# Expert stage of a hybrid RWKV-7/GLA/MoE layer: gates and float32r parts in the copies of w2's sums, scatter within the next pair, other terms of y in the tenth pair, branch in the fourteenth

## Chip, cores and metric

The kernel runs on 1 core of one Trainium2 chip. The metric is the device time of one execution in microseconds (us), the median of several runs. Engines are named as in the profile: PE is TensorE's matmul side and PEld its weight loads, DVE is VectorE, ACT is ScalarE, POOL is GpSimd, SP is SyncE, whose queue issues the weight transfers.

## What is computed

One encoder layer for 256 tokens of width 1024: an RWKV-7 and a GLA mixer, then a top-4-of-32 mixture of experts, each followed by a layer norm of alpha times the residual plus the result. The change lies in the mixture of experts:

```
logits = xt @ router_w + router_b
top_val, top_idx = lax.top_k(logits, 4)
gate = softmax(top_val)
for each expert e, for the tokens that chose it:
    h = xt[tok] @ w1[e] + b1[e]                     # 1024 -> 2048
    gt = minimum(h[:, :1024], 7); up = clip(h[:, 1024:], -7, 7)
    act = (up + 1) * gt * sigmoid(1.702 * gt)
    o = act @ w2[e] + b2[e]                         # 1024 -> 1024
    y[tok] += gate * o
x = layer_norm(alpha * x + y)
```

All 32 experts' weights are float32 and are read from memory once: w1 is 8 MB an expert, w2 4 MB.

## The kernel before

The mixing stage (to about 240 us) ends in the router (`out_route`, `choose`). The expert stage is a loop over 16 **pairs** of experts, `e2` 0 to 15. Each expert takes up to 64 of its tokens, so that the two of a pair fill 128 columns.

Weights arrive through a **ring of ten slots** of 2 MB (`fetch`, L284), filled by SP's queue in the order of the stream: for each pair eight slots of w1 and four of w2. SP issues a transfer only when PE has read the last of what stood in its slot.

Within a pair PE does, in the order of the program:

- **Gather** (L1264): `so`, a 0/1 matrix of tokens by places, times the normalised tokens; ACT (L1099) and DVE (L1100) copy the result out of PSUM to `xg` with the norm's gain.
- **Transposes of sg** (L1286): `so` times the gates is `sg` (DVE); its transpose `sgT` is copied by ACT (L1287).
- **w1** (L1310), 16 instructions a slot, with the bias at L1314; `swiglu` (DVE, ACT) and four transposes (L1090) give `aT`.
- **w2** (L1332), 16 instructions a slot. There is one PSUM bank for its sums (`bo`); ACT copies the lower 64 rows to `oc` (L1334), DVE the upper 64 (L1335), and the second expert's w2 waits for the first's copies.
- **Scatter** (L1339): `sgT` times `oc`, float32, four matmuls of 128x512 in eight instructions, each sum added to `y` by DVE (L1340). It waits for the second expert's copies, and the next pair's gather stands behind it.

`init_y` (L1223 to L1234) writes y's other terms, alpha times the residual and the gate times b2, in pair 0 between the two experts of w2. At pair 6 stands `overflow` (L1120 to L1122): a branch with a loop for experts with more than 64 tokens, which all engines pass, SP among them. From pair 2 on a row of parameters for the last norm lies in `oh` (L1212, on SP's queue, behind `init_y`, which reads the same tile).

In the last pair (15) w2 is read in pieces of 256 columns (L1363): even pieces sum into a bank `o`, odd ones into a bank `x`; ACT copies each to `oq` (L1365), and its scatter (L1368) and DVE's addition to `y` follow. Then come the norm and the output.

A scheduler sets the order of instructions on each engine, by its own estimate of times; it also takes w1's matmuls of the two experts in turn where `xg` comes late.

Of the kernel before, what the change touches and what calls it, by code (L numbers as in the profile page):

```python
# [137 lines left out]
def mix_moe(ctx: ExitStack, tc: tile.TileContext, A, out, dbg=None):  # L138
# [1103 lines left out]

    gained = [None, None]
    for e2 in range(NE // 2):
# [32 lines left out]
        sgT = mo.tile([128, 2, T], F32, name="sgT", tag="sgT")  # L1277
        pb = bank("x")
        for v in range(2):
            for t in range(2):  # L1280
                o = pb[:, v * T + t * 128:v * T + (t + 1) * 128]
                if last:
                    for h in range(2):
                        PE.matmul(o[64 * h:64 * h + 64], lhsT=sg[:, t, v], rhs=ident, start=True, stop=True)
                else:
                    PE.transpose(o, sg[:, t, v:v + 2].rearrange("p a b -> p (a b)"), ident)  # L1286
        S.activation(sgT.rearrange("p a b -> p (a b)"), pb, AF.Copy)  # L1287
        if last:

            ln2 = xres  # L1290
            for i in range(4):
                pb = bank("x")
                for h in range(2):
                    row(pb[:, h * 256:(h + 1) * 256], rt, 2 * i + h)
                S.activation(ln2[:, i // 2, i % 2 * 512:i % 2 * 512 + 512], pb, AF.Copy)
# [146 lines left out]
```

## Time and profile before

| | us |
|---|---|
| median of 3 runs (lowest, highest) | 1199.7 (1198.8, 1199.85) |
| the profiled execution's own time | 1194.37 |
| its span, first to last instruction | 1192.5 |
| PE busy (matmuls; their ends are modelled) | 1092.7 |
| DVE busy | 391.3 |
| ACT busy | 200.6 |
| read from memory | 426.67 MB |

The profiled execution is 5.3 us shorter than the median of the runs. Busy time of PE is no measure of need here: an engine that waits for data only at some slots shows as busy in the rest. The DMA line of the profile's second part is the mean busy share of the core's 16 DMA engines in 40 slices of 29.8 us, in tenths (9 is 90% or more), and the GB/s line under it is what they moved.

### The profile page before, as it was taken

The page shows a single profiled execution, that of the slowest core. Times are in us where ns is not written, and L with a number is a line of the kernel's source. Part 1 is how long each engine was busy: PE and PEld are TensorE (multiplying, and loading weights), DVE is VectorE, ACT ScalarE, POOL GpSimd, SP SyncE. Part 2 cuts the span into 40 slices and gives each one's busy share as a digit, 9 for nine tenths or more (in the row PEclk, how much of TensorE's full clock was granted, in tenths as well). Part 3 has the DMA queues.
Part 4 walks back from the last instruction along what each step waited for, and adds up shares of the span by engine and source line. Part 5 has one row for each costly group of instructions (what it writes and reads, how often), then busy time and mean ns, then how long its engine had stood idle before and what let it go on. Part 6 is the DMA issues. An engine that isn't in the chain of part 4 may idle for free.

```text
span 1192.5 us, 14141 instructions
## 1 busy us (share of the span) xinstructions
PE 1092.7 (92%) x5964; PEld 528.8 (44%) x5964; DVE 391.3 (33%) x792; ACT 200.6 (17%) x368; POOL 83.9 (7%) x75
## 2 busy tenths in 40 slices
PE   8889899999999999999899999999899999998995
PEld 5679787643434343433333333333333333333443
DVE  7767976424222221221212222212222222222125
ACT  5544322111011111110101010110101010101111
POOL 4605610010000000000000000000000000000001
PEclk9879999998999999999999999999999999999998
DMA  9211364689799999999989999999999999999991
GB/s 336 115 71 72 142 255 166 249 346 428 285 429 428 428 429 427 427 428 429 425 357 430 425 429 429 427 426 428 429 428 428 427 428 427 428 426 428 426 400 43
DMA packets 36201, 428.68 MB, mean 359 GB/s; under 512 B 3947, under 2 KB 6276, under 8 KB 9382
## 3 DMA queue, kind: packets, MB, share of 16 engines
q1 hardware_dynamic: 35362, 426.41, 85.5%
q10 hardware_dynamic: 772, 1.32, 0.3%
q8 instruction: 48, 0.79, 0.3%
q14 instruction: 19, 0.16, 0.0%
HBM read 426.67 MB, written 1.05 MB: 359 GB/s over the span
## 4 chain that ended last, share of the span: by engine, by line
PE 28%; DMA 19%; DVE 2%; ACT 1%; issue 0%; DVEq 0%; ACTq 0%
DMA slot<-w 19%; PE bg L1310 13%; PE bo L1332 5%; PE bx L1264 4%; PE bx L1339 3%; DVE oc L1335 1%; PE bx L1368 1%; ACT oc L1334 1%; PE bx L1363 1%; PE bo L1363 1%; PE bx L1090 0%; PE bx L1286 0%; PE bx L1217 0%; DVE y L1391 0%; PE bg L1314 0%
## 5 line engine op out<-in xcount | busy, mean ns | idle before, releaser
L1310 PE MATMUL bg<-slot,xg 128*64 128x512 f32 x2048 | 462.0, 596 | 0.0
L1310 PEld LDWEIGHTS bg<-slot,xg 128*64 128x64 f32 x2048 | 140.7, 137 | 250.8 <-issue 236.2
L1332 PE MATMUL bo<-slot,aT 128*64 128x512 f32 x960 | 218.4, 601 | 35.0 <-DVE oc L1335 16.3
L1332 PEld LDWEIGHTS bo<-slot,aT 128*64 128x64 f32 x960 | 68.1, 138 | 168.4 <-issue 114.8
L1082 DVE TENSOR_SCALAR gt<-bg 128x512 f32<-128x512 f32 x32 | 22.1, 691 | 284.7 <-PE bg L1314 284.7
L1264 PEld LDWEIGHTS bx<-so,xres 128*128 128x128 f32 x512 | 67.8, 196 | 49.4 <-issue 46.4
L1335 DVE COPY oc<-bo 64x512 f32<-64x512 f32 x30 | 20.8, 694 | 205.2 <-ACT oc L1334 205.1
L1264 PE MATMUL bx<-so,xres 128*128 128x128 f32 x512 | 79.4, 292 | 1.1 <-DVEq L1121 1.1
L1100 DVE TENSOR_SCALAR xg<-bx,cst 128x128 f32<-128x128 f32 x64 | 26.2, 410 | 162.0 <-PE bx L1264 111.6
L1339 PE MATMUL bx<-oc,sgT 128*128 128x512 f32 x120 | 55.5, 605 | 21.3 <-DVE oc L1335 21.3
L1083 ACT ACTIVATE up<-gt 128x512 f32<-128x512 f32 x32 | 20.1, 629 | 312.1 <-DVE gt L1082 312.1
L1410 POOL TENSOR_TENSOR y<-y,xres 128x512 f32<-128x512 f32 x1 | 1.4, 1442 | 917.9 <-ACT y L1409 917.9
L1099 ACT ACTIVATE xg<-bx,cst 128x128 f32<-128x128 f32 x64 | 28.6, 457 | 173.8 <-PE bx L1264 170.8
L401 PE MATMUL bp<-xth,whi 128*128 128x256 f32 x144 | 45.0, 313 | 6.9 <-DVE slot L430 6.9
L1340 DVE TENSOR_TENSOR y<-bx,y 128x512 f32<-128x512 f32 x60 | 41.5, 692 | 25.8 <-PE bx L1339 25.8
L1334 ACT ACTIVATE oc<-bo 64x512 f32<-64x512 f32 x30 | 17.7, 591 | 186.9 <-PE bo L1332 179.5
L403 PE MATMUL bp<-xth,wlo 128*128 128x256 f32 x144 | 43.7, 305 | 3.6 <-DVE wlo L391 3.6
L1339 PEld LDWEIGHTS bx<-oc,sgT 128*128 128x128 f32 x120 | 21.6, 189 | 56.0 <-DVE oc L1335 34.5
L402 PE MATMUL bp<-xtl,whi 128*128 128x256 f32 x144 | 43.5, 303 | 0.0
L391 DVE TENSOR_TENSOR wlo<-slot,whi 128x512 fp32r<-128x512 f32 x37 | 35.7, 974 | 19.0 <-ACT whi L388 18.9
L388 ACT ACTIVATE whi<-slot 128x512 fp32r<-128x512 f32 x50 | 31.2, 629 | 49.6 <-PE bp L402 27.2
L1092 ACT ACTIVATE aT<-bx 128x512 f32<-128x512 f32 x32 | 19.1, 597 | 121.5 <-PE bx L1090 121.4
(419 smaller groups left out, 1020.6 us busy)
## 6 DMA issues: line engine op xcount, KB each, us to landing
slot<-w SPq DMA_DIRECT2D x188, 2048.0 KB, 34.1
slot<-win SPq DMA_DIRECT2D x12, 1024.0 KB, 7.8
slot<-w2l SPq DMA_DIRECT2D x7, 1024.0 KB, 33.2
slot<-wout SPq DMA_DIRECT2D x4, 1024.0 KB, 7.6
slot<-win SPq DMA_DIRECT2D x3, 512.0 KB, 6.8
slot<-lora SPq DMA_DIRECT2D x1, 1024.0 KB, 11.0
slot<-rows SPq DMA_DIRECT2D x2, 512.0 KB, 13.9
y<-b SPq DMA_DIRECT2D x4, 256.0 KB, 13.2
```

Of the source, the lines that this page charges most:

```text
L388: S.activation(hi, src, AF.Copy)
L391: (eng if b is None else (V, G)[b]).tensor_tensor(lo, src, hi.bitcast(F32), op=OP.subtract)
L401: PE.matmul(ps, lhsT=hi[:, k, :], rhs=xth[:, kk, :], start=(kk == 0), stop=False)
L402: PE.matmul(ps, lhsT=hi[:, k, :], rhs=xtl[:, kk, :], start=False, stop=False)
L403: PE.matmul(ps, lhsT=lo[:, k, :], rhs=xth[:, kk, :], start=False, stop=(kk == 7))
L1264: i = PE.matmul(pb[:, j * 128:(j + 1) * 128], lhsT=xres[:, t, c0:c0 + 255:2], rhs=so[:, t].rearrange("p a b -> p (a b)"), start=(t == 0), ...
L1310: PE.matmul(pp[64 * hf:64 * hf + 64, :], lhsT=lt, rhs=w[:, c0 + 512 * hf:c0 + 512 * hf + 512], start=(k == 0), stop=False)
L1332: PE.matmul(po[64 * half:64 * half + 64, :], lhsT=aTs[i][:, j, 64 * hf:64 * hf + 64], rhs=w[:, c0:c0 + 512], start=(f == 0), stop=(f == 7))
L1334: S.activation(oc[0:64, i, :], po[0:64], AF.Copy)
L1335: V.tensor_copy(oc[64:, 1 - i, :], po[64:])
L1339: PE.matmul(pb, lhsT=sgT[:, g, t * 128:(t + 1) * 128], rhs=oc[:, g, :], start=True, stop=True)
L1340: V.tensor_tensor(y[:, t, g * 512:(g + 1) * 512], pb, y[:, t, g * 512:(g + 1) * 512], op=OP.add)
```

## The change

- The gates leave the scatter's left side. `so`, not `sg`, is transposed, into a float32r tile `soT` (0 and 1 are exact in it). Small matmuls with two columns pick each place's gate out of `gate`, and DVE's two-column sums put it in `gp` [128, 2].
- The copies of w2's sums multiply by the gate. ACT writes the product as float32r (`oc[:, 0]`), DVE writes the rest, product minus that part, as float32r too (`oc[:, 1]`). Both do both halves of the rows, so there are four copies an expert where there were two.
- The scatter is eight float32r matmuls of 128x512 (two parts for each of four blocks), and it stands in the next pair's w1, behind the first expert's k = 1. The first one writes `y` by a copy (ACT); later ones add as before.
- `bo` has two PSUM banks, `x` two where it had three.
- The transposes of `aT` stand later: the first expert's within the second's w1, the second's within the first's w2.
- `init_y` runs in the tenth pair (`e2 == 9`) and adds to `y`; `oh`'s parameters are loaded in the twelfth.
- `overflow` stands at `e2 == 13`, behind the scatter of pair 12.
- In the last pair `sg`, its transposes and the norm's parameters stay, in another place: behind the first expert's w1.
- `_build` sets `dynamic_dma_scratch_size=1024`, which leaves more of SBUF to tiles.

```diff
-    banks.update({"g": 4, "x": 3, "o": 1})
+    banks.update({"g": 4, "x": 2, "o": 2})
...
+    def scatter(soT, ocs, start):
+        for g in range(2):
+            for t in range(2):
+                pb = bank("x")
+                for h in range(2):
+                    PE.matmul(pb, lhsT=soT[:, g, t * 128:(t + 1) * 128], rhs=ocs[g][:, h], start=(h == 0), stop=(h == 1))
+                o = y[:, t, g * 512:(g + 1) * 512]
+                if start:
+                    S.activation(o, pb, AF.Copy)
+                else:
+                    V.tensor_tensor(o, pb, o, op=OP.add)
...
-        if e2 == 6:
+        if e2 == 13:
+            scatter(*pending)
+            pending = None
             overflow()
...
-        for t in range(2):
-            V.tensor_tensor(sg[:, t, 0:2], so[:, t], gq[:, t], op=OP.mult)
-            V.tensor_copy(sg[:, t, 2], sg[:, t, 0])
...
+                if i == 0 and k == 1 and pending:
+                    scatter(*pending)
+                    pending = None
+                if i == 1 and k == 4:
+                    aTs.append(transposed(ups[0]))
...
+                soT = mo.tile([128, 2, T], F32R, name="soT", tag="sgT")
+                gp = mo.tile([128, 2], F32, name="gp", tag="gp", bufs=2)
+                for v in range(2):
+                    pb = bank("x")
...
+                            PE.transpose(pb[:, t * 128:(t + 1) * 128], s2, ident)
+                            PE.matmul(pb[:, T + 2 * t:T + 2 * t + 2], lhsT=s2, rhs=gs_, start=True, stop=True)
...
+                    S.activation(soT[:, v], pb[:, 0:T], AF.Copy)
...
-        if e2 == 0:
+        if e2 == 9:
             G.memset(gT[NE:NE + 1], 1.0)
...
             init_y()
...
-            S.activation(oc[0:64, i, :], po[0:64], AF.Copy)
-            V.tensor_copy(oc[64:, 1 - i, :], po[64:])
-        for t in range(2):
-            for g in range(2):
-                pb = bank("x")
-                PE.matmul(pb, lhsT=sgT[:, g, t * 128:(t + 1) * 128], rhs=oc[:, g, :], start=True, stop=True)
-                V.tensor_tensor(y[:, t, g * 512:(g + 1) * 512], pb, y[:, t, g * 512:(g + 1) * 512], op=OP.add)
+                if i == 0 and f == 6:
+                    with tc.issue_after(o.ins):
+                        aTs.append(transposed(ups[1]))
+            for half in range(2):
+                hs = slice(64 * half, 64 * half + 64)
+                oc = ocs[half ^ i]
+                S.activation(oc[hs, 0], po[hs], AF.Copy, scale=gp[hs, i:i + 1])
+                V.scalar_tensor_tensor(oc[hs, 1], po[hs], gp[hs, i:i + 1], oc[hs, 0].bitcast(F32), op0=OP.mult,
+                                       op1=OP.subtract)
+        pending = (soT, ocs, e2 == 0)
```

What the scheduler makes of it on PE, at three places. First, the end of pair 0 and the start of pair 1, before (L1332 is w2, L1223 to L1233 `init_y`, L1339 the scatter, L1264 the next gather, L1310 w1):

```order
L1332 MATMUL bo<-slot,aT 64x512 x16
L1090 MATMUL bx<-cst,up 128x128 x4
L1223 MATMUL bx<-cst,gate 32x128 x2
L1228 MATMUL bx<-b2t,oh 128x512
L1233 MATMUL bx<-b2t,oh 128x512 x2
...
L1332 MATMUL bo<-slot,aT 64x512 x16
L1339 MATMUL bx<-oc,sgT 128x512 x4
L1264 MATMUL bx<-so,xres 128x128 x4
```

and changed (L1379 is w2, L1283 the gather, L1304 w1, L1254 the scatter):

```order
L1093 MATMUL bx<-cst,up 128x128 x4
L1379 MATMUL bo<-slot,aT 64x512 x16
L1093 MATMUL bx<-cst,up 128x128 x4
L1283 MATMUL bx<-so,xres 128x128 x2
L1379 MATMUL bo<-slot,aT 64x512 x16
L1283 MATMUL bx<-so,xres 128x128 x4
L1304 MATMUL bg<-slot,xg 64x512 x8
```

Nothing stands between the two experts' w2 now but the transposes and a piece of the next gather; `init_y` is gone from here, and the scatter stands later, within pair 1's w1.

Second, the end of pair 14 and the start of pair 15, before (L1284 transposes sg in the last pair, L1217 spreads the norm's parameters):

```order
L1332 MATMUL bo<-slot,aT 64x512 x24
L1339 MATMUL bx<-oc,sgT 128x512 x4
L1264 MATMUL bx<-so,xres 128x128 x4
L1284 MATMUL bx<-cst,sg 64x128 x8
L1264 MATMUL bx<-so,xres 128x128 x2
L1310 MATMUL bg<-slot,xg 64x512 x4
```

and changed (L1328 and L1220 are those two):

```order
L1283 MATMUL bx<-so,xres 128x128 x8
L1379 MATMUL bo<-slot,aT 64x512 x8
L1283 MATMUL bx<-so,xres 128x128 x8
L1379 MATMUL bo<-slot,aT 64x512 x8
L1304 MATMUL bg<-slot,xg 64x512 x8
L1254 MATMUL bx<-oc,soT 128x512 x6
L1304 MATMUL bg<-slot,xg 64x512 x8
L1254 MATMUL bx<-oc,soT 128x512 x2
L1328 MATMUL bx<-cst,sg 64x128 x2
```

The gather of pair 15 moved ahead of the last two slots of pair 14's w2, and behind the last slot w1 starts at once, with the scatter behind its first slot.

Third, the start of the last w2, before (numbers tell buffers apart: bo_6151, bx_6165 and bo_6179 are pieces 0, 1 and 2, bx_6161, bx_6175 and bx_6189 their scatters):

```order
L1363 MATMUL bo_6151<-slot_6029,aT_6092 64x256 x8
L1368 MATMUL bx_6161<-oq_6150,sgT_6002 128x256 x2
L1363 MATMUL bx_6165<-slot_6029,aT_6092 64x256 x8
L1363 MATMUL bo_6179<-slot_6032,aT_6092 64x256 x8
L1368 MATMUL bx_6175<-oq_6150,sgT_6002 128x256 x2
L1368 MATMUL bx_6189<-oq_6150,sgT_6002 128x256 x2
```

and changed (pieces bo_6441, bx_6455, bo_6469; scatters bx_6451, bx_6465, bx_6479):

```order
L1413 MATMUL bo_6441<-slot_6273,aT_6404 64x256 x8
L1418 MATMUL bx_6451<-oq_6440,sgT_6348 128x256 x2
L1413 MATMUL bo_6469<-slot_6276,aT_6404 64x256 x8
L1413 MATMUL bx_6455<-slot_6273,aT_6404 64x256 x8
L1418 MATMUL bx_6465<-oq_6440,sgT_6348 128x256 x2
L1418 MATMUL bx_6479<-oq_6440,sgT_6348 128x256 x2
```

Piece 2 now stands ahead of piece 1, and piece 1's scatter directly behind piece 1; the same holds of the three pairs of pieces that follow.

## Rows read from the trace of the kernel before

**Rows 1.** The page's 40 slices of 29.8 us.

```profile
DMA  9211364689799999999989999999999999999991
GB/s 336 115 71 72 142 255 166 249 346 428 285 429 428 428 429 427 427 428 429 425 357 430 425 429 429 427 426 428 429 428 428 427 428 427 428 426 428 426 400 43
```

**Rows 2.** Issues of transfers: count, KB each, median us to landing.

```profile
slot<-w SPq DMA_DIRECT2D x188, 2048.0 KB, 34.1
```

**Rows 3.** PE's timeline, w2's last slot of pairs 12 and 13: start, us, [idle before].

```profile
986.89 3.65 PE L1332 MATMUL bo<-slot,aT 128*64 128x512 f32 x16 [1.00 <-DMA slot<-w]
...
1045.92 3.65 PE L1332 MATMUL bo<-slot,aT 128*64 128x512 f32 x16 [0.99 <-DMA slot<-w]
```

**Rows 4.** Stretches of 5 us: busy PE, PEld, DVE, ACT, POOL; PEclk, DMA share, GB/s.

```profile
245.00:250.00 5.00, 5.00 (x26) 2.06 (x24) 0.41 (x1) 0.46 (x1) 2.06 (x1) 1.00 0.40 139
250.00:255.00 5.00, 5.00 (x24) 1.74 (x20) 0.41 (x1) 0.00 (x0) 0.71 (x1) 1.00 0.76 256
...
300.00:305.00 5.00, 5.00 (x24) 1.48 (x21) 0.00 (x0) 0.00 (x0) 0.00 (x0) 0.92 0.63 202
...
310.00:315.00 5.00, 5.00 (x30) 2.95 (x30) 1.67 (x3) 1.47 (x3) 0.00 (x0) 1.00 0.73 315
315.00:320.00 5.00, 5.00 (x28) 2.19 (x26) 0.41 (x1) 0.46 (x1) 0.00 (x0) 1.00 0.00 0
...
615.00:620.00 5.00, 4.87 (x24) 1.91 (x24) 0.42 (x1) 0.60 (x1) 0.00 (x0) 1.00 0.22 95
```

**Rows 5.** SP's timeline: issues from 285 to 322 us.

```profile
302.19 19.10 SPq L284 DMA_DIRECT2D slot<-w  x4
```

**Rows 6.** PE's timeline of init_y in pair 0.

```profile
286.47 0.38 PE L1223 MATMUL bx<-cst,gate 128*32 128x128 f32 x2
...
296.30 1.12 PE L1332 MATMUL bo<-slot,aT 128*64 128x512 f32 x2 [1.51 <-DVE oc L1335]
```

**Rows 7.** Stretches of 4 us around the same place, and 5 us of pair 6.

```profile
290.00:294.00 4.00, 4.00 (x6) 1.20 (x5) 2.52 (x4) 0.00 (x0) 0.00 (x0) 0.56 1.01 430
294.00:298.00 4.00, 2.49 (x5) 0.53 (x6) 1.39 (x2) 0.59 (x1) 0.00 (x0) 0.50 1.02 434
...
635.00:640.00 5.00, 3.55 (x18) 1.27 (x20) 0.69 (x1) 0.59 (x1) 0.00 (x0) 1.00 1.02 436
```

**Rows 8.** SP's waits, 580 to 622 us: total, times, longest.

```profile
SPq L1121 <- SPq L1121: 32.3, 3, 22.5
```

**Rows 9.** PE's timeline, end of pair 14 and start of pair 15.

```profile
1105.41 3.65 PE L1332 MATMUL bo<-slot,aT 128*64 128x512 f32 x16 [1.16 <-DMA slot<-w]
1110.48 3.70 PE L1339 MATMUL bx<-oc,sgT 128*128 128x512 f32 x8 [1.42 <-DVE oc L1335]
1114.02 1.10 PE L1264 MATMUL bx<-so,xres 128*128 128x128 f32 x8
1115.05 1.09 PE L1284 MATMUL bx<-cst,sg 128*64 128x128 f32 x16
```

**Rows 10.** The mixing stage's float32r matmuls of 256 columns, and float32 ones of two.

```profile
66.04 0.28 PE L403 MATMUL bp<-xth,wlo 128*128 128x256 f32 x1
66.16 0.28 PE L401 MATMUL bp<-xth,whi 128*128 128x256 f32 x1
...
67.60 1.17 PE L532 MATMUL ba<-cstm,slot 128*128 128x2 f32 x10
```

**Rows 11.** The timeline, pair 15: the last w2 and its copies.

```profile
1154.91 1.90 PE L1363 MATMUL bo<-slot,aT 128*64 128x256 f32 x16
...
1161.94 1.90 PE L1363 MATMUL bo<-slot,aT 128*64 128x256 f32 x16
1163.77 1.99 PE L1368 MATMUL bx<-oq,sgT 128*128 128x256 f32 x8
1163.89 0.38 ACT L1365 ACTIVATE oq<-bo 128x256 f32<-128x256 f32 x1 [1.34 <-PE bo L1363]
...
1165.69 0.65 PE L1363 MATMUL bx<-slot,aT 128*64 128x256 f32 x4
```

More of the change, by code (lines that the diff above doesn't have):

```diff
@@ L1086, in swiglu, with transposed @@
         V.scalar_tensor_tensor(up, up, 1.0, gt, op0=OP.add, op1=OP.mult)
+        return up
+    def transposed(up, step=4):
         pb = bank("x")
@@ L1272, in mix_moe @@
                 nc.gpsimd.dma_start(dbg["gate"], gate.rearrange("p a b -> p (a b)"))
-        for t in range(2):
-            V.tensor_tensor(sg[:, t, 0:2], so[:, t], gq[:, t], op=OP.mult)
-            V.tensor_copy(sg[:, t, 2], sg[:, t, 0])
-        sgT = mo.tile([128, 2, T], F32, name="sgT", tag="sgT")
-        pb = bank("x")
-        for v in range(2):
-            for t in range(2):
[L1281 to L1295, printed above, removed]
-        if e2 == 1:
-            rt = oh.rearrange("p a e c -> p (a e c)")[0:8]
-            rows(rt, "ln2w", nc.sync)
         b0 = 2 + 12 * e2
         aTs = []
+        ups = []
         for i in range(2):
@@ L1317, in mix_moe @@
+        if e2 == 11:
+            rt = oh.rearrange("p a e c -> p (a e c)")[0:8]
+            rows(rt, "ln2w", nc.sync)
         if last:
+            aTs.append(transposed(ups[1]))
             break
-        if e2 == 0:
+        if e2 == 9:
             G.memset(gT[NE:NE + 1], 1.0)
@@ L1323, in mix_moe @@
             init_y()
-        oc = mo.tile([128, 2, 512], F32, name="oc", tag="oc")
+        ocs = [mo.tile([128, 2, 512], F32R, name="oc", tag=("oc", "oc1")[g]) for g in range(2)]
         for i in range(2):
@@ L1331, in mix_moe @@
                     c0 = 512 * (half ^ i)
-                    PE.matmul(po[64 * half:64 * half + 64, :], lhsT=aTs[i][:, j, 64 * hf:64 * hf + 64],
-                              rhs=w[:, c0:c0 + 512], start=(f == 0), stop=(f == 7))
-            S.activation(oc[0:64, i, :], po[0:64], AF.Copy)
-            V.tensor_copy(oc[64:, 1 - i, :], po[64:])
-        for t in range(2):
-            for g in range(2):
-                pb = bank("x")
-                PE.matmul(pb, lhsT=sgT[:, g, t * 128:(t + 1) * 128], rhs=oc[:, g, :], start=True, stop=True)
-                V.tensor_tensor(y[:, t, g * 512:(g + 1) * 512], pb, y[:, t, g * 512:(g + 1) * 512], op=OP.add)
-    st = mo.tile([128, 2, 5, 6], F32, name="st2")
+                    o = PE.matmul(po[64 * half:64 * half + 64, :], lhsT=aTs[i][:, j, 64 * hf:64 * hf + 64],
+                                  rhs=w[:, c0:c0 + 512], start=(f == 0), stop=(f == 7))
+                if i == 0 and f == 6:
+                    with tc.issue_after(o.ins):
+                        aTs.append(transposed(ups[1]))
+            for half in range(2):
[5 more added lines that the diff above has]
+        pending = (soT, ocs, e2 == 0)
+    st = mo.tile([128, 2, 5, 6], F32, name="st2", tag="gt")
     mv = mo.tile([128, 2, 2], F32, name="mv2")
```

53 lines of the change are left out of this document (43 added, 10 removed).

## The prediction
> **What bounds the kernel now.** Read the page's DMA and GB/s lines first [rows 1]. From the thirteenth slice on (357 us) the 16 DMA engines are full and move 427 to 430 GB/s, but for one slice of 357 and the end. A slot of 2048 KB [rows 2] therefore takes 2.097 MB / 427 GB/s = 4.9 us, a pair of twelve 58.9 us. PE's last w2 slot of pair 12 starts at 986.89 and that of pair 13 at 1045.92, 59.0 us apart, each after a wait for its transfer of 1.0 us [rows 3]. So the expert stage goes at the pace of the transfers, and PE, nine tenths busy, has about 1 us a pair to spare. PE time saved in a middle pair turns into a longer wait for the next slot and is worth nothing.
>
> What can be won lies where the transfers stop, and behind the last one. The transfers stop in three places [rows 4], each priced as 5 us times the missing share:
>
> - 245 to 255: 3.0 + 1.2 = 4.2 us, at the first w1 slots of pair 0.
> - 300 to 320: 1.85 + 1.35 + 5.0 = 8.2 us, at the change from pair 0 to pair 1.
> - 615 to 620: 3.9 us, at the branch of pair 6.
>
> The second place has a visible cause. SP issues at 302.19 and then just three times in 19 us [rows 5]: it waits for PE to free slots. PE was late because `init_y` sat between the two experts of w2, from 286.47 to 296.30, 9.8 us [rows 6], and in it the granted clock fell from 1.00 to 0.50, the lower of the two levels, 1.2 GHz [rows 7].
>
> Behind the last transfers PE sets the time. Its last wait for a slot ends at 1105.41 [rows 9]; from there to the end it is PE's own work, and the last w2 starts at 1154.91 [rows 11], 49.5 us later.
>
> **The change part by part.**
>
> *`init_y` out of pair 0.* In the new order nothing of it stands between the experts of w2. PE loses there its 9.8 us and the wait for the single bank's copies (1.51 us, in the last row of [rows 6]), and the scatter of 3.5 us (1114.02 - 1110.48 [rows 9]) stands later. Pair 0 gains the `soT` work of about 1.9 us (below) for the 0.5 of sg's transposes. The slots that SP got at 302.19 come free some 10 us earlier, before the transfers run dry at about 301; the first slots of pair 1 follow at 3.65 us each against 4.9 that the transfers need, so PE keeps ahead. I take the whole **8.2 us** as won. Bounds: 0 if another wait takes its place, 8.2 at most; nearest the upper end, because PE leads by several us where the transfers need the slots.
>
> *The first hole, 245 to 255.* PE's order up to there is the same in both kernels. Nothing.
>
> *The branch, pair 6 to pair 13.* SP's waits at it add up to 32.3 us, the longest 22.5 [rows 8]: it issues nothing until what it had issued is down, and then the engines stand empty, 3.9 us. SP's order around the branch is the same, two w2 slots of the pair ahead of it, so I expect the same hole 412 us (7 x 58.9) later. Worth nothing, as the transfers bind on both sides of it. Bounds 0 to 3.9 us won, none to 2 lost; I take 0.
>
> *The middle pairs.* Per pair PE loses the scatter's float32 (3.5) for eight float32r matmuls of 512 columns: one of 256 takes 0.12 us from start to start [rows 10], so 8 x 0.24 = 1.9. It loses two waits for copies (1.42 in [rows 9], and one like the 1.51) and sg's four transposes (0.5, half of the eight of half width that take 1.09 in [rows 9]). It gains `soT`: two transposes and four matmuls of half width, about 0.9 by the same row, and six with two columns, 12 instructions of at most 0.12 [rows 10], 0.9 to 1.4. Net 3.5 + 2.9 + 0.5 - 1.9 - 1.9 to 2.3 = about 3 us less. By the pace of the transfers this is worth nothing, but PE's spare time grows from 1.0 to about 4 us a pair. ACT and DVE get two more copies of 64 rows an expert; both are three quarters idle or more, and with two `bo` banks no w2 waits for them.
>
> Here a row meets a rule. Share and GB/s are flat in every slice between the holes, and slots, not PE, end the waits [rows 1, 3]. The Trainium skill, "Perfetto Trace Analysis", section "Identifying the Most-Contended Engine", calls the occupancy of the 16 DMA engines misleading and would look at the memory's use instead. If it were misleading here and PE set the pace, all 3 us of each of 15 pairs would come out; that is rival 3.
>
> *`init_y` in the tenth pair.* It puts PE up to 9.8 us behind [rows 6]. The ring holds free slots then, as PE waits for transfers, and pairs 10 to 12 give back 3 x 4 us. Worth nothing. The load of `oh` on SP's queue waits for it, behind slots that wait for the same pair's w1 anyway: nothing.
>
> *The scatter ahead of the branch.* In pair 13 the scatter and the gather stand in the open: copies about 2 us, scatter 1.9, gather 4.4 (8 of its 32 instructions take 1.03, 1115.05 - 1114.02 [rows 9]), 8 to 9 us. The hole delays the transfers by 3.9, pairs 13 and 14 give 4 each: made up.
>
> *The end.* Take 0 as the start of pair 14's last w2 slot; w1's eight slots of pair 15 then land at 4.9, 9.8, ..., 39.2. In the new order PE ends that slot at 3.65, waits to 4.9, does the first slot to 8.6, six scatter matmuls to 10.4 (DVE's addition of 0.7 frees the second bank of x late), the second slot to 14.1, two scatter matmuls to 14.6. Then `sg`, which shares `oc1`'s room, is written late: about 1 us, its transposes 1.1, one row of parameters 1.05 (to 17.7). Slots three and four with two rows (2.1) lead to 27, bias and the last row to 28.5, and the remaining four slots, 14.6, the transposes 0.7 and the bias 0.4 to **44.1**. Before, it took 49.5, since scatter, gather and a 1.42 us wait stood in front of w1. Won: 5.4 us.
>
> Against that stands the order of the last w2. Before, piece 1's copy (0.38) ran beside piece 2's matmuls, and the scatter followed without a gap: 1161.94, 1163.77, 1165.69 [rows 11]. Now piece 1 stands directly ahead of its own scatter. PE must wait for ACT's start (0.12 after the matmuls, 1163.89 - 1163.77), 0.38, and a little: 0.55 us, four times, **2.2 us**. The end keeps 5.4 - 2.2 = **3.2 us**. Bounds: 1.5, if `sg`'s wait is longer; 5.4, if the copies hide.
>
> **Sum.** 8.2 + 3.2 = 11.4 us off the profiled execution's 1194.4: 1183.0. The median of the runs stands 5.3 above that execution, so it is 1199.7 - 11.4 = **1188.3 us**.
>
> **Rivals.**
>
> 1. *The hole at 300 us stays, wholly or half.* For it: SP's queue is in order, and one late slot holds all behind it. Against it: the slots are free several us early. With half of it left 1188.3 + 4.1 = 1192.4; with all of it only the end is won, 1196.5.
> 2. *Slower: PE's clock falls after its waits, and PE becomes the bound.* PE now waits 4 us a pair in short pieces, and the gates' matmuls have two columns. In [rows 7] the clock fell to 0.50 in matmuls of few rows; a fall of 8 us costs 4 us of lag (8 us at half speed do 4 us of work). One fall a pair is paid by the spare 4 us; it decides from there on. Two falls a pair, 8 us, leave 4 us over in each of 14 pairs: 1188.3 + 56 = 1244; one and a half, 2 over: 1216. Against it: at 635 to 640 PE was busy for 3.55 of 5 us with the clock at 1.00 [rows 7]. The Trainium skill, "TensorE: Matmul & The Clock Gate", section "HAM oscillation — how this bites in real kernels", says that waits for transfers can throw the engine back to the lower clock again and again; by that rule this rival would be the likely one, and the row at 635 us speaks against it. A single fall in pair 15, where nothing pays it back, gives 1192.3.
> 3. *PE set the pace all along.* 15 x 3 us more: 1188.3 - 45 = 1143. Against it stands the flat GB/s line [rows 1].
> 4. *No change.* The stream hides all: the hole at 300 us moves to another place (the tenth pair, where `init_y` now stands, or a larger one at the branch) and the last w2's gaps eat the rest: 1199.7.
>
> **Numbers.** Forecast (1188.3; by its bounds, 5.4 for 3.2 at the end and up to 3 of the branch's hole gone on one side, 1.5 at the end and 2 lost at the branch on the other: 1183 to 1192) 0.73. Rival 1 with the single fall of rival 2: 0.12, most of it below 1196. Rival 4: 0.08. Rival 2: 0.04. Rival 3: 0.03. A measurement of this kernel tells 0.2% from no change, 2.4 us: under 1197.3 is faster, over 1202.1 slower. Faster: 0.73 + 0.12 + 0.03 = 0.88; within 0.08; slower 0.04. The range of 1183 to 1196 holds the forecast and most of rival 1.
>
> **What would show it.** Right: a share of 1.00 from about 255 us to the branch, one hole of about 4 us near 1020 us, SP's waits at the branch as before, the last landing 8 us earlier; PE's waits for slots up to 4 us a pair; about 44 us from pair 14's last slot to the last w2, and gaps of 0.5 us ahead of four of its scatters. Wrong in the first term: a hole at 290 to 330 us or in pair 10. Wrong in the second: 49 us again, or a clock of 0.50 in pair 15. The forecast fails altogether if PE's waits for slots don't grow: then PE was the bound, or has become it.

## The result and the profile after

| | before | changed |
|---|---|---|
| median of 4 runs each, on one chip (us) | 1199.25 | 1184.08 |
| lowest, highest (us) | 1193.3, 1199.85 | 1179.43, 1186.18 |
| span of the profiled execution (us) | 1192.5 | 1181.9 |

The ratio is 0.9879 with a 95% interval of 0.9836 to 0.9922. The change is faster by some 15 us in the medians and by 10.6 us between the two profiled executions. Predicted were 1188.3 us and 11.4 us. In three later rounds, each on one chip, the kernel before had medians of 1195.4 (16 runs), 1194.8 (12) and 1194.6 us (11), so the four runs of it in this table stand 4 to 5 us high. Against 1195 the changed kernel's 1184.1 would be 0.991; this estimate sets one round against another, and the 10.6 us between the profiled executions fit it.

The changed page's DMA and GB/s lines, 40 slices of 29.5 us, answer to [rows 1]:

```profile
DMA  9312364589999999999999999999999999799992
GB/s 336 119 72 76 139 258 158 241 337 429 427 428 428 429 426 428 427 427 429 427 426 429 428 427 426 429 428 426 427 428 428 426 429 426 322 428 427 428 418 63
```

The slice of 285 GB/s near 310 us is gone, and the line is flat at 426 to 429 GB/s from the tenth slice (266 us) on, but for one slice and the end. The slice of 357 has become one of 322, in the place to which the branch was moved. The stretches of 5 us (columns as in [rows 4]) show both:

```profile
245.00:250.00 5.00, 5.00 (x26) 2.07 (x24) 0.41 (x1) 0.46 (x1) 2.77 (x1) 1.00 0.22 93
250.00:255.00 5.00, 5.00 (x23) 1.63 (x19) 0.41 (x1) 0.00 (x0) 0.00 (x0) 1.00 0.81 282
300.00:305.00 5.00, 5.00 (x24) 2.05 (x22) 0.41 (x1) 0.46 (x1) 0.00 (x0) 1.00 1.01 429
310.00:315.00 5.00, 5.00 (x22) 1.75 (x21) 0.00 (x0) 1.05 (x2) 0.00 (x0) 1.00 1.00 419
315.00:320.00 5.00, 5.00 (x25) 1.90 (x22) 0.00 (x0) 0.00 (x0) 0.00 (x0) 1.00 1.01 429
...
1010.00:1015.00 5.00, 5.00 (x40) 2.45 (x38) 3.80 (x10) 1.18 (x3) 0.00 (x0) 1.00 0.99 423
1015.00:1020.00 5.00, 5.00 (x26) 2.05 (x24) 0.00 (x0) 0.60 (x1) 0.00 (x0) 1.00 0.60 256
1020.00:1025.00 5.00, 5.00 (x26) 1.69 (x24) 0.00 (x0) 0.00 (x0) 0.00 (x0) 1.00 0.14 56
1025.00:1030.00 5.00, 5.00 (x28) 1.70 (x26) 2.56 (x4) 0.63 (x1) 0.00 (x0) 1.00 0.98 351
```

In this section and the next a hole is priced by its last column: the GB/s missing against 429, times 5 us, over 429. At the branch that is (6 + 173 + 373 + 78) x 5 / 429 = 7.3 us.

PE's timeline from pair 14's w2 to the end (start, us, [idle before]) answers to [rows 9, 11]:

```profile
1082.13 3.65 PE L1379 MATMUL bo<-slot,aT 128*64 128x512 f32 x16 [0.90 <-DMA slot<-w]
1086.93 2.79 PE L1379 MATMUL bo<-slot,aT 128*64 128x512 f32 x12 [1.15 <-DMA slot<-w]
...
1097.36 2.50 PE L1283 MATMUL bx<-so,xres 128*128 128x128 f32 x16
1099.79 3.65 PE L1379 MATMUL bo<-slot,aT 128*64 128x512 f32 x16
...
1108.56 0.74 PE L1254 MATMUL bx<-oc,soT 128*128 128x512 f32 x2 [0.55 <-DVE y L1259]
...
1114.53 0.44 PE L1328 MATMUL bx<-cst,sg 128*64 128x128 f32 x4 [0.98 <-DVE sg L1324]
...
1142.22 1.90 PE L1413 MATMUL bo<-slot,aT 128*64 128x256 f32 x16
...
1151.64 1.99 PE L1418 MATMUL bx<-oq,sgT 128*128 128x256 f32 x8 [0.48 <-ACT oq L1415]
...
1157.72 1.99 PE L1418 MATMUL bx<-oq,sgT 128*128 128x256 f32 x8 [0.48 <-ACT oq L1415]
...
1163.87 1.99 PE L1418 MATMUL bx<-oq,sgT 128*128 128x256 f32 x8 [0.54 <-ACT oq L1415]
...
1168.13 1.16 PE L1418 MATMUL bx<-oq,sgT 128*128 128x128 f32 x8 [0.38 <-ACT oq L1415]
```

From pair 14's last slot to the last w2 there are now 1142.22 - 1099.79 = 42.4 us, where there were 49.5. That slot starts only 5.6 us earlier than before (1105.41 in [rows 9]). The four gaps ahead of the last scatters are there, 1.9 us together.

### The profile page after: what moved, and what is told of

Its sections match the earlier page's. It is cut to its first block, busy times and chain, and to the rows that moved or that the text cites. A ratio compares the mean times of both kernels' runs of the same rounds, so it can differ in the third digit from the quotient of the medians.

```text
span 1181.9 us, 14744 instructions
## 1 busy us (share of the span) xinstructions
PE 1097.3 (93%) x6234; PEld 545.0 (46%) x6234; DVE 414.1 (35%) x820; ACT 227.8 (19%) x417; POOL 84.3 (7%) x75
## 5 line engine op out<-in xcount | busy, mean ns | idle before, releaser
L1304 PE MATMUL bg<-slot,xg 128*64 128x512 f32 x2048 | 469.6, 598 | 4.9 <-DMA slot<-w 4.9
L1304 PEld LDWEIGHTS bg<-slot,xg 128*64 128x64 f32 x2048 | 147.9, 137 | 262.4 <-issue 244.9
L1379 PE MATMUL bo<-slot,aT 128*64 128x512 f32 x960 | 219.0, 597 | 13.2 <-DMA slot<-w 11.2
L1379 PEld LDWEIGHTS bo<-slot,aT 128*64 128x64 f32 x960 | 65.3, 136 | 129.4 <-issue 106.7
L1388 DVE SCALAR_TENSOR_TENSOR oc<-bo,gp,oc 64x512 fp32r<-64x512 f32 x60 | 45.0, 750 | 163.4 <-ACT oc L1387 163.0
L1283 PEld LDWEIGHTS bx<-so,xres 128*128 128x128 f32 x512 | 67.5, 199 | 52.3 <-issue 44.1
L1283 PE MATMUL bx<-so,xres 128*128 128x128 f32 x512 | 82.1, 300 | 8.4 <-PEq L1124 6.3
L1259 DVE TENSOR_TENSOR y<-bx,y 128x512 f32<-128x512 f32 x56 | 37.4, 689 | 81.5 <-PE bx L1254 81.5
L1387 ACT ACTIVATE oc<-bo,gp 64x512 fp32r<-64x512 f32 x60 | 41.0, 683 | 93.3 <-PE bo L1379 82.8
L1254 PE MATMUL bx<-oc,soT 128*128 128x512 f32 x120 | 40.4, 436 | 9.5 <-DVE y L1259 7.2
L1355 ACT ACTIVATE soT<-bx 128x256 fp32r<-128x256 f32 x30 | 11.5, 384 | 142.9 <-PE bx L1349 132.1
```

Of the source, the lines that this page charges most:

```text
L1254: PE.matmul(pb, lhsT=soT[:, g, t * 128:(t + 1) * 128], rhs=ocs[g][:, h], start=(h == 0), stop=(h == 1))
L1259: V.tensor_tensor(o, pb, o, op=OP.add)
L1283: i = PE.matmul(pb[:, j * 128:(j + 1) * 128], lhsT=xres[:, t, c0:c0 + 255:2], rhs=so[:, t].rearrange("p a b -> p (a b)"), start=(t == 0), ...
L1304: PE.matmul(pp[64 * hf:64 * hf + 64, :], lhsT=lt, rhs=w[:, c0 + 512 * hf:c0 + 512 * hf + 512], start=(k == 0), stop=False)
L1379: o = PE.matmul(po[64 * half:64 * half + 64, :], lhsT=aTs[i][:, j, 64 * hf:64 * hf + 64], rhs=w[:, c0:c0 + 512], start=(f == 0), stop=(f = ...
L1387: S.activation(oc[hs, 0], po[hs], AF.Copy, scale=gp[hs, i:i + 1])
```

## The experiments

Four spots of each trace are compared throughout: PE's start of pair 1's second w2 (where the holes at 245 and 300 us lie behind it), of pair 14's last w2 slot, of the last w2, and the end of the span. The first takes out where an execution's mixing stage ended, which differs by up to 8 us. All are from PE's timeline of one profiled execution each:

| kernel | branch at pair | pair 1 to 14's last slot | to the last w2 | to the end | pair 1 to the end |
|---|---|---|---|---|---|
| changed | 13 | 753.6 | 42.4 | 39.7 | 835.7 |
| branch6 | 6 | 752.1 | 42.4 | 39.6 | 834.1 |
| tail_order | 13 | 751.9 | 42.4 | 37.7 | 832.1 |
| branch6_tail | 6 | 753.0 | 44.1 | 37.7 | 834.8 |
| branch4_tail | 4 | 752.2 | 44.1 | 37.6 | 834.0 |
| nobranch | none | 747.6 | 44.1 | 39.4 | 831.1 |
| scatter_f32 | 13 | 751.5 | 43.8 | 39.6 | 835.0 |
| after_sg | 13 | 753.3 | 43.0 | 39.6 | 835.9 |
| best_sg | 6 | 753.5 | 43.0 | 37.7 | 834.2 |

Under each kernel stand its expectation and the median of its runs. Ratios are to the kernel before in the same round (before_init9, init0, branch6 and tail_order in the first; nobranch, branch4_tail, branch6_tail and scatter_f32 in the second; the two with `sg` in the third), with the 95% interval in brackets.

### The hole at 300 us: `init_y` alone, forth and back

before_init9 is the kernel before with `init_y`, and the `oh` load behind it, moved to where the change has them. What that needs comes with it: the first scatter writes `y` by a copy, `b2t` gets room of its own, and `dynamic_dma_scratch_size=1024` frees it. The main lines:

```diff
-        if e2 == 1:
+        if e2 == 11:
...
-        if e2 == 0:
+        if e2 == 9:
...
             init_y()
```

> The kernel before, with one part of the change alone: y's other terms (init_y) in the tenth pair, the first scatter copies into y, the norm's parameters loaded in the twelfth pair. My theory: the transfers' hole at 300 to 320 us came from init_y between the experts of w2 alone, so it is gone, 20 MB from the 30th to the 50th MB of the stream take 47 us instead of 57, and the last w2 starts about 10 us earlier: span 1182.5, with the hole at pair 6 as before (4.7 us) and 49.5 us of own work of TensorE at the end. Rival (the scatter and the copies freed the slots): a hole of over 4 us stays at 300 to 320 us and the span is above 1186.

Measured: median 1186.5 us, ratio 0.9923 (0.9884 to 0.9962), span 1184.7, between the theory's 1182.5 and the rival's 1186. The hole at 300 us is gone; the stretches there and at the branch:

```profile
300.00:305.00 5.00, 5.00 (x29) 2.36 (x28) 0.47 (x2) 0.77 (x2) 0.00 (x0) 1.00 0.99 423
...
310.00:315.00 5.00, 5.00 (x25) 1.91 (x26) 1.02 (x4) 0.05 (x1) 0.00 (x0) 1.00 1.03 436
315.00:320.00 5.00, 5.00 (x26) 1.73 (x24) 0.83 (x5) 0.00 (x0) 0.00 (x0) 1.00 0.99 419
...
600.00:605.00 5.00, 4.86 (x26) 1.76 (x22) 2.17 (x4) 1.23 (x2) 0.00 (x0) 1.00 0.90 383
605.00:610.00 5.00, 5.00 (x26) 1.71 (x24) 0.00 (x0) 0.00 (x0) 0.00 (x0) 1.00 0.26 93
610.00:615.00 5.00, 5.00 (x28) 1.69 (x26) 0.42 (x1) 0.00 (x0) 0.00 (x0) 1.00 0.96 347
```

The last w2 starts 9.5 us earlier than before (1145.44 for 1154.91), near the 10 expected. From there to the end it takes 39.3 us for 37.6: behind a wait of 1.85 us at 1149.18 the clock fell, which cost 1.7 us. So `init_y` alone is worth 7.8 us between the profiled executions, about 9.5 without that fall, and all the rest of the change together 1 to 3 of the 10.6.

init0 is the changed kernel with `init_y` back in pair 0, where it again writes `y` first:

```diff
-        if e2 == 9:
+        if e2 == 0:
...
-        pending = (soT, ocs, e2 == 0)
+        pending = (soT, ocs, False)
```

> The changed kernel with init_y back in pair 0 (it writes y, every scatter adds). My theory: most of the hole at 300 us is back, since TensorE frees the slots of the second expert's w2 some 7 to 10 us later; two bo banks and the later scatter give back about 4 us of TensorE's lead, so the hole is 4 to 8 us by GB/s and the span 1181.9 + 4 to 8 = 1186 to 1190. Rival (two bo banks and the later scatter alone hide init_y): no hole, span 1182.

Measured: median 1197.53 us (1188.67 to 1203.88), ratio 0.9997 (0.9958 to 1.0036). The hole is back, later and spread, and so is the clock's fall in `init_y`:

```profile
300.00:305.00 5.00, 5.00 (x16) 2.33 (x16) 1.23 (x2) 1.05 (x2) 0.00 (x0) 0.53 0.99 423
305.00:310.00 5.00, 5.00 (x26) 1.56 (x24) 0.00 (x0) 0.00 (x0) 0.00 (x0) 1.00 0.61 179
...
315.00:320.00 5.00, 5.00 (x24) 2.05 (x22) 0.41 (x1) 0.46 (x1) 0.00 (x0) 1.00 0.84 360
320.00:325.00 5.00, 5.00 (x23) 1.86 (x20) 0.41 (x1) 0.00 (x0) 0.00 (x0) 1.00 0.84 288
```

Summed over all its stretches from 305 to 360 us, 8.8 us are missing, more than the 4 to 8 expected; the two `bo` banks and the later scatter hid about 1 of the 9.9 us that are missing before, not 4. The span of 1195.6 is above the expected 1186 to 1190, but about 5 us of it are not `init_y`'s: the mixing stage ran at a lower clock (last section). The ten runs lie in two groups, four at 1188.7 to 1190.7 and six at 1197.4 to 1203.9, and the profile is of the second. Moving `init_y` alone wins 0.8% where the whole change has 1.2%. That the ratio of init0 is 1 is in part the mixing stage; its hole is `init_y`'s. Both directions name the same part, and no other wait took the hole's place.

### The branch: position, and none

branch6 puts the branch back to the seventh pair (`e2 == 6`), with all else changed:

> The changed kernel with the branch at pair 6 instead of 13. The hole at the branch took 7.3 us of the stream with the branch at 13 and 4.7 before with it at 6. Theory A: the 16 DMA engines drift apart with the time since they last stood empty together (763 us with the branch at 13, 295 us before), and a queue that is drained costs that drift: at pair 6 they last stood empty at 252 us, 350 us earlier, so the hole is 4.7 to 5.3 us and the last w2 starts 2 to 2.5 us earlier. Rival B: the hole is larger because TensorE is not behind when SP reaches the branch, so eight transfers are out: 7.3 us here only if TensorE stands equally close, and with TensorE behind (it first waits for a slot at 717 us) about 4.7 as well; then a third place tells. Rival C: the hole does not depend on the place: 7.3 us, span as with 13.

Measured: median 1182.91 us, ratio 0.9891 (0.9843 to 0.9938), within the interval of the changed kernel. Its hole is 4.6 us, and the last w2 starts 1.9 us earlier (1140.28 for 1142.22), 1.5 counted from pair 1. By the bytes rival C falls; theory A and rival B expect about the same here.

nobranch leaves the branch and its loop out, so tokens beyond an expert's 64 are not computed, and the scatter of pair 12 stands in pair 13's w1 again:

```diff
-        if e2 == 13:
-            scatter(*pending)
-            pending = None
-            overflow()
```

> The changed kernel with the branch and its loop left out (no expert's tokens beyond 64 are computed), and the scatter back in the next pair's w1 there. Theory: the branch stops the transfers because SP issues nothing until all in flight has landed; the loss is 5.6 to 7.3 us of stream by volume in the thirteenth pair, and PE follows the stream. Expected: no stretch under 400 GB/s between 330 us and the last landing, span 1174 to 1176.5 against 1181.9 for the changed kernel. Rival: PE is the bound in the last pairs and would have needed that time anyway; then PE's stall at the branch (8 to 9 us) goes, but its end comes no more than 2 us earlier, span 1180 to 1182.

Measured: median 1177.98 us, ratio 0.9872 (0.9797 to 0.9948), span 1175.0. One of its four runs took 1191.14, and the interval holds the changed kernel's ratio, so what the branch costs is read from the profile alone. No stretch under 400 GB/s is left between pair 0 and the end of the stream, and pair 14's first w2 slot arrives earlier:

```profile
1073.90 3.65 PE L1377 MATMUL bo<-slot,aT 128*64 128x512 f32 x16 [0.90 <-DMA slot<-w]
```

Counted from pair 1 (343.94 here, 346.22 in the changed kernel), that is 730.0 against 735.9 us: PE gets the data 5.9 us earlier. Both kernels wait 0.90 us for this slot, so PE had made up its own stall at the branch by then. So of the 7.3 us that the stream lost at the branch 5.9 reach PE. The trace of the changed kernel shows why it stops: SP issues nothing from 983.23 to 1024.03 us, and the last transfer that it had issued lands at 1023.81; before, it is 586.05 to 619.22, with the last landing at 618.7. The span was in the range of the theory, but for mixed reasons: 2.3 us come from an earlier pair 1, and 1.6 were given back in pair 15 by a fall of the clock (below). The rival, that PE would have needed the time anyway, falls by the 5.9 us.

branch4_tail has the branch at `e2 == 4` and the order of the next part:

> The changed kernel with the branch at the fifth pair (e2 == 4) and the last w2's pieces in numeric order. Theory that the 16 engines drift apart with the time since they were last empty, and that the hole grows with it (4.4 to 5.3 us at pair 6, 5.6 to 7.3 at pair 13): hole of 3.5 to 4.5 us by volume near 485 us, gaps of the last w2 gone, span 1176.5 to 1179. Rival, the hole is the same wherever the branch stands: hole 5.5 to 7 us, span 1179 to 1181.

Measured: median 1184.63 us (1179.37 to 1191.55), ratio 0.9915 (0.9878 to 0.9951), span 1179.4. Its hole is 5.0 us (174 and 259 GB/s at 485 to 495 us), above the range of the drift theory (3.5 to 4.5) and below its rival's (5.5 to 7); neither is met. Priced in the same way, the holes of all kernels are 5.0 at pair 4; 4.9, 5.4, 4.6, 5.4 and 6.0 at pair 6; 7.3, 5.7, 6.9, 6.6 and 6.9 at pair 13. So the hole does not grow from pair 4 to pair 6, and in pair 13 it is about 1.4 us longer in the mean, with 5.7 to 7.3 close above 4.6 to 6.0. That the engines drift apart with time is one reading of it and is not shown. Rival B of branch6 is another: at pairs 4 and 6 PE works off its backlog, and SP's wait at the branch comes in two or three pieces, while at pair 13 it comes in seven. PE's time, moreover, shows no price of the place: from pair 1 to pair 14's last slot the table has 752.1 to 753.5 us with the branch at pair 4 or 6 and 751.5 to 753.6 at 13. The scatter in the open ahead of the branch does not explain it, since branch6 and branch4_tail have it too. This stays open.

PE's own stall at the branch did change with the kernel, and not with the place:

```profile
989.09 2.97 PE L1283 MATMUL bx<-so,xres 128*128 128x128 f32 x12 [6.32 <-PEq L1124]
```

It is 5.7 to 6.5 us in all eight kernels of the changed form that have a branch besides this one, at pair 4, 6 and 13 alike, and 1.1 in the kernel before and in before_init9. Why was not tried. Three small transfers of the profile's instruction queues pass in these 6.3 us, so a wait of PE for its own program is possible; it is not shown. The 0.90 us that PE waits for pair 14's first slot, with the branch and without it, say that this stall is made up by then.

### The order of the last w2

tail_order makes each piece wait for the piece before it in the program's order, so that a piece's copy again runs beside the next one's matmuls:

```diff
+    piece = None
...
-            with tc.issue_after(sums[-2].ins) if len(sums) > 1 else ExitStack():
+            with tc.issue_after(sums[-2].ins) if len(sums) > 1 else ExitStack(), \
+                    tc.issue_after(piece.ins) if piece else ExitStack():
...
-                    PE.matmul(po[64 * half:64 * half + 64, :], lhsT=aTs[i][:, k, 64 * hf:64 * hf + 64],
+                    piece = PE.matmul(po[64 * half:64 * half + 64, :], lhsT=aTs[i][:, k, 64 * hf:64 * hf + 64],
```

> The changed kernel with one order forced: in the last w2 the even piece's matmuls stand behind the odd piece's, as before the change. My theory: the four gaps of 0.48, 0.48, 0.54 and 0.38 us ahead of the scatters go, TensorE's part from the last w2's first matmul to its last scatter takes 24.5 instead of 26.4 us, the span is 1.9 us shorter (about 1180.0). Rival: with two x banks the odd piece then waits for DVE to free a bank, gaps of 0.3 to 0.6 us stand ahead of the odd pieces instead and nothing is won.

Measured: median 1182.07 us, ratio 0.989 (0.9839 to 0.9942), span 1179.0. The four gaps are gone, none stands in their place, and the last part takes 37.7 us for 39.7. It does so in all four kernels with this order, to 0.1 us: 2.0 us is what the changed order costs.

branch6_tail joins this with the earlier branch:

> The changed kernel with the branch back at the seventh pair (e2 == 6) and the last w2's pieces in numeric order. If the two gains add up (2 us for the branch, 1.9 for the gaps): span 1178, median about 1179. Rival, the end of the two is the same work and one hides the other: span 1179.5 to 1181.

Measured: median 1181.12 us, ratio 0.9859 (0.9808 to 0.991), span 1180.3, at the rival's value, though not for the rival's reason. The 2.0 us were won and, from pair 1 to pair 14's last slot, 0.6 of the 2 expected of the branch, but pair 15 took 44.1 us for 42.4 and gave 1.6 back.

### A fall of the clock in pair 15

The 1.6 us of branch6_tail lie in one stretch (columns as above; the clock is the last but two):

```profile
1110.00:1114.00 4.00, 3.02 (x16) 1.08 (x13) 1.09 (x3) 0.00 (x0) 0.00 (x0) 1.00 1.01 426
1114.00:1118.00 4.00, 4.00 (x22) 2.24 (x22) 0.00 (x0) 1.19 (x2) 0.00 (x0) 0.57 1.00 426
1118.00:1122.00 4.00, 4.00 (x21) 1.85 (x18) 0.00 (x0) 0.24 (x1) 0.00 (x0) 1.00 1.01 430
```

For most of 4 us the lower level, 1.2 GHz, was granted. Ahead of it PE had stood still for 0.55 and 0.98 us and then done sg's transposes and the parameters' matmuls of 8 rows. branch4_tail and nobranch show the same 1.6 us; the changed kernel, with the same order of instructions and the same waits there, and tail_order and branch6 don't. after_sg gives `sg` a room that nothing uses any more, so that it does not wait for the scatter; best_sg is branch6_tail with the same edit:

```diff
-                sg = mo.tile([128, 2, 2, 64], F32, name="sg", tag="oc1")
+                sg = mo.tile([128, 2, 2, 64], F32, name="sg", tag="tmp")
```

> The changed kernel with nothing but sg's room changed. Its profile had no fall of the clock in the last pair, so only the wait of 0.98 us is to be won: 41.4 us from pair 14's last w2 slot to the last w2 (42.4 before this edit), span 1181 if the branch's hole is 7.3 us again, 1179.3 if it is 5.6. Rival, another wait takes its place (the scatter's second bank, DVE's additions ahead of the next copies): 42.4 us again.

> Branch at the seventh pair, pieces of the last w2 in numeric order, and the last pair's sg in a room of its own (that of tmp, which nothing uses after the tenth pair) in place of oc1's. Theory: sg's wait of 0.98 us for the scatter is what lets the clock fall to about 0.59 for some 4 us in the last pair of three of the kernels so far; with the wait gone both go. From the start of the fourteenth pair's last w2 slot (pair 14 of 0 to 15) to the last w2: 41.4 us (42.4 without a fall, less 0.98), clock 1.00 throughout, span 1177.5 to 1178.5. Rival, the short matmuls themselves (transposes of sg, rows of parameters) bring the fall, not the wait: a stretch near 0.6 stays, 43 us, span 1179 to 1180.

Measured: after_sg 1181.5 us, ratio 0.988 (0.9841 to 0.9918); best_sg 1185.96 us (1177.35 to 1190.6), ratio 0.9893 (0.9851 to 0.9935). In both pair 15 takes 43.0 us, where 41.4 was expected of both. The span of best_sg, 1186.0, is above both its ranges, since its mixing stage ran long (last section). The wait of 0.98 is gone, and the scheduler puts six of the parameters' matmuls in a row; behind them the clock falls, here in after_sg:

```profile
1110.55 1.09 PE L1328 MATMUL bx<-cst,sg 128*64 128x128 f32 x16
...
1116.21 2.94 PE L1220 MATMUL bx<-oh,cst 8*128 8x256 f32 x12
1119.08 5.35 PE L1304 MATMUL bg<-slot,xg 128*64 128x512 f32 x16
```

Sixteen matmuls of w1 that take 3.65 us took 5.35, 1.7 more. So a fall does not need that wait, and the rival's 43 us are right: PE was busy without a gap from 1107 to 1119 us and the clock fell all the same, behind matmuls of 8 rows. That these bring it is not shown either: the changed kernel, tail_order and branch6 have them too, four in a row in place of six, and no fall there. What decides between two executions stays open.

### The float32r parts

scatter_f32 undoes them: `soT` and `oc` in float32, one part, two copies an expert for four, four float32 scatter matmuls for eight float32r ones.

```diff
-                for h in range(2):
-                    PE.matmul(pb, lhsT=soT[:, g, t * 128:(t + 1) * 128], rhs=ocs[g][:, h], start=(h == 0), stop=(h == 1))
+                PE.matmul(pb, lhsT=soT[:, g, t * 128:(t + 1) * 128], rhs=ocs[g][:, 0], start=True, stop=True)
```

> The changed kernel with the float32r parts undone: soT and oc in float32, one part, the first half of the rows copied by ACT and the second by DVE, four float32 scatter matmuls in place of eight float32r ones. All else as changed. Theory, the transfers set the pace of the middle pairs and PE time saved there is worth nothing: span 1180 to 1184 (at most 2 us at the end, where one scatter stands in the last pair behind the last waits). Rival, PE sets the pace, and its 1.6 us more a pair (3.5 for 1.9) come out in 14 pairs: span 1200 to 1206.

Measured: median 1183.52 us, ratio 0.9885 (0.9833 to 0.9937), span 1180.8. PE gets slower, 55.7 us a pair for 54.1 (half of 575.71 - 464.31, below, against half of 571.14 - 462.85 in the next section), and the time does not move: the span is in the theory's 1180 to 1184, far from the rival's 1200 to 1206.

```profile
464.31 3.65 PE L1378 MATMUL bo<-slot,aT 128*64 128x512 f32 x16
...
575.71 3.65 PE L1378 MATMUL bo<-slot,aT 128*64 128x512 f32 x16
```

From pair 1 to pair 14's last slot it takes 751.5 us, 2 us less than the changed kernel. Only in pair 15, where one scatter stands behind the last wait, it pays 1.4 us (43.8 for 42.4). And yet PE of this kernel has not one wait for a slot between 340 and 1060 us.

## Why the prediction was right, and where its steps failed

**The hole at 300 us.** The mechanism holds in both directions. The term was 8.2 us; it is 9.9. In [rows 4] the stretches from 300 to 320 us and that of 320 to 325 (347 GB/s in the same view) lack 227 + 114 + 429 + 82 GB/s. The step that failed is the pricing by the share: it counts the time that packets take, and at the edges of the hole they take longer for their bytes (a share of 0.63 at 202 GB/s, and 0.98 at 347 in the stretch behind the hole, which was left out).

**The branch.** Taken as 0, bounded at 2 lost. The hole went from 4.9 us by the same pricing (3.9 by the share) to 7.3, so 2.4 were lost in the stream, just past the bound. In PE's time the place of the branch shows no price (the table), and there the 0 held. "I expect the same hole" failed in its size: in the changed kernel the 16 DMA engines run dry over two stretches (share 0.60, then 0.14), before in one (0.22). SP's waits, expected as before, were 8 us longer: 40.2 us in seven pieces, the longest 9.3, in the place of 32.3 in three.

**The end.** Predicted 44.1 us from pair 14's last slot to the last w2, measured 42.4; predicted 2.2 us of gaps, measured 1.9 and 2.0 with them removed. The working assumed that PE ends the slot and waits 1.25 us for the next. In fact PE was late, since 2.5 us of pair 15's gather stood directly in front of that slot. The stream ends some 8 us earlier (worked out from 311 GB/s in 1150 to 1155 us, which is 1153.6, against 380 and 172 in 1155 to 1165 before, which is 1161.4) and the slot starts only 5.6 us earlier; part of the 49.5 us was moved ahead of the slot and not removed. By the prediction's points: 5.6 for the slot, + 7.1 for pair 15, - 2.1 for the last w2 = 10.6 us, the measured difference of the spans. Put in the prediction's terms, by the stream: 9.9 for the hole, less 2.4 at the branch, leaves 3.1 for the end, where 3.2 stood. This 3.1 is what is left over, and no run has the new end alone. That the total came so near is luck: two errors of about 2 us had opposite signs.

**From 1183.0 to the median.** The 11.4 us off the profiled execution gave 1183.0 and came to 1183.7. The forecast of the median added the 5.3 us by which three runs of the kernel before stood above its profiled execution; the changed kernel's median stands only 0.4 above its own. That is the whole of the 4.2 us by which the forecast was too high.

**The middle pairs.** Worth nothing, as predicted, and shown by scatter_f32. But the numbers behind it were off. PE's own pace can be read where it works through slots that are already full, last slots of w2 two pairs apart. Before:

```profile
466.32 7.09 PE L1332 MATMUL bo<-slot,aT 128*64 128x512 f32 x32 [1.48 <-DVE oc L1335]
...
578.92 7.09 PE L1332 MATMUL bo<-slot,aT 128*64 128x512 f32 x32 [1.48 <-DVE oc L1335]
```

and changed:

```profile
462.85 3.65 PE L1379 MATMUL bo<-slot,aT 128*64 128x512 f32 x16
...
571.14 3.65 PE L1379 MATMUL bo<-slot,aT 128*64 128x512 f32 x16
```

That is 56.3 us a pair before and 54.1 changed: 2.2 us saved, not 3, and a spare of 2.6 us before (58.9 - 56.3), not 1.0. The lines of three pairs (430 to 600 us; busy us, mean ns, idle before) show where the estimate was short, before:

```profile
L1332 PE MATMUL bo<-slot,aT 128*64 128x512 f32 x192 | 43.0, 595 | 4.4 <-DVE oc L1335 4.4
...
L1339 PE MATMUL bx<-oc,sgT 128*128 128x512 f32 x24 | 11.1, 605 | 4.3 <-DVE oc L1335 4.3
```

and changed:

```profile
L1254 PE MATMUL bx<-oc,soT 128*128 128x512 f32 x24 | 8.0, 434 | 1.7 <-DVE y L1259 1.7
...
L1353 PE MATMUL bx<-cst,so 128*64 128x128 f32 x24 | 2.4, 294 | 0.8 <-DVE y L1259 0.8
L1349 PE MATMUL bx<-gate,so 128*128 128x2 f32 x12 | 1.7, 210 | 0.0
L1348 PE MATMUL bx<-cst,so 128*128 128x128 f32 x6 | 1.7, 288 | 0.0
L1354 PE MATMUL bx<-gate,so 128*64 128x2 f32 x24 | 1.5, 183 | 0.0
```

The two waits for copies went as priced: 8.7 us in three pairs, 2.9 a pair. `soT` takes 7.3 us in three pairs, 2.4 a pair, where 1.9 to 2.3 stood; its transposes and half-width matmuls take 1.4 of it, where 0.9 stood. The float32r scatter takes 8.0, 2.7 a pair, where 1.9 stood. The 0.12 us of [rows 10] did carry over: in a run the matmuls of 512 columns start 0.23 us apart (472.30, 472.53 and 472.77 in the trace). What the estimate missed is that the scatter comes in three runs a pair, each with 0.34 us to its second matmul and 0.39 for its last. The scatter waits 0.57 us a pair for `x`'s second bank, as foreseen for pair 15 alone, and `soT` 0.27 more. (A run ends some 0.17 us behind the start of the next, so busy times of many short runs add up to too much; the pace is the measure.)

"The forecast fails altogether if PE's waits for slots don't grow": this test was badly chosen. Such waits begin only when PE has worked off the backlog from pair 0, at 809 us before and 712 changed. They then come to 3.6 us in 700 to 760 us and, in nobranch, 3.8 in 1000 to 1060, the 4 us foreseen. But `init_y` in the tenth pair and the branch put PE behind again. Before, 820 to 1060 us have 2.0 to 4.0 us of them per 60 us, and changed 940 to 1000 us has 5.2, so the rise is small. The reading of [rows 3] that PE had "about 1 us a pair to spare" took one wait of a pair for all of them.

**The rivals.** Rival 1 (the hole stays) fell with the first fence. Rival 3 (PE set the pace) fell with scatter_f32, where 1.6 us more in each of 14 pairs would have made 22 us and made none. The Trainium skill's warning that the occupancy of the DMA engines misleads was right in another way than was weighed: the share put the holes at 8.2 and 3.9 us where bytes, with the stretches beside them, put them at 9.9 and 4.9. Of rival 2 a single fall of the clock in pair 15 is real: it costs 1.6 to 1.7 us where 4 were priced, and came in five of the nine profiled executions of the table. In the middle pairs of the changed kernel no wait for a slot brought a fall: from 340 to 1060 us its clock is below 1.00 only in the tenth pair (0.57 in 770 to 774 us, in `init_y`) and at the branch (0.55 in 985 to 990, 0.76 in 990 to 995). In tail_order one did:

```profile
890.76 8.78 PE L1304 MATMUL bg<-slot,xg 128*64 128x512 f32 x32 [1.92 <-DMA slot<-w]
```

These 32 matmuls take 7.09 us at full clock, and 0.57 was granted in 891 to 895 us. In before_init9 a wait of 2.79 us at 1090.81 shows the same. Behind waits of 1.67 and 2.07 us before, and of 1.74 in nobranch, the clock stayed at 1.00. By the Trainium skill ("TensorE: Matmul & The Clock Gate", the section that the prediction names) waits for transfers bring such falls. These two agree with it; in after_sg no wait of any kind was needed. The section's example has one long wait in each round of a loop, where the changed kernel waits for slots in pieces of 0.3 to 1.3 us, so the rule did not make this rival likely.

Rival 4's tenth pair shows no hole; its branch and its gaps took 2.4 and 2.0 us.

**What is best.** branch6_tail and after_sg have the lowest medians with a branch, 1181.12 and 1181.5 us. Against the changed kernel's ratio of 0.9879 their 0.9859 and 0.988 are the same within the intervals, and no version is shown to beat it. By the table the order of the last w2 is worth 2.0 us in each profile.

## What to carry to other kernels

Look for the places where a saturated stream stops, price each by the bytes missing and not by the busy share, and change what stands in front of it; PE time saved between them was worth nothing here. Whether an engine has time to spare is read from its pace while its input is ready, not from its waits: an engine that works off a backlog shows no wait, and is still not the bound. Moving a stall (here a branch that all queues pass) does not remove it: the hole was 4.6 to 7.3 us wherever the branch stood, and only the kernel without it lost none.

## What the runs showed that was not expected

- The granted clock of the mixing stage differs between executions of one order of work, and where it is low the whole stream starts later. The first 100 us of the changed kernel and then of best_sg, which have the same code there (columns as above):

```profile
0.00:100.00 100.00, 84.09 (x517) 68.80 (x518) 71.81 (x120) 51.91 (x94) 39.33 (x38) 0.91 0.48 177
```

```profile
0.00:100.00 100.00, 82.64 (x465) 68.41 (x466) 65.90 (x111) 50.53 (x92) 36.12 (x36) 0.83 0.45 161
```

  At 0.83 pair 1's second w2 starts at 351.80 for 346.22 us; init0 had 0.83 too. These 5.6 us are about what the whole branch costs PE (5.9), and the reason that the spots in the table are counted from pair 1. What lowers the clock there is not shown.
- The clock can fall while PE is busy without a gap: in after_sg 1.7 us were lost behind six matmuls of 8 rows. And one and the same wait, 1.84 to 1.85 us behind the first piece of the last w2, was followed by a fall in before_init9 and by none in the eleven other profiles.
- The scatter's eight instructions take 434 ns each as float32r and 605 as float32 (the lines of three pairs, above). But in a run a float32r one starts every 0.23 us and a float32 one every 0.43, so that in a long run two float32r parts take about half the time of one float32 matmul (two instructions). The scatter, in its three short runs a pair, got it down to seven tenths.
